# A rotary embedding whose tables are built from 64 partitions instead of 128, with the first unit loaded in one piece

## Chip, cores and metric

One core of a Trainium2 chip. The metric is the device time of one execution in microseconds (us). Each kernel was run several times, in turns with the kernel before on the same chip.

## The reference

```python
# x: (8, 8, 1024, 64) float32; cos_cached, sin_cached: (1024, 32) float32
x_first, x_second = x[..., :32], x[..., 32:]
out_first  = x_first * cos_cached - x_second * sin_cached
out_second = x_first * sin_cached + x_second * cos_cached
out = concatenate([out_first, out_second], axis=-1)
```

16.8 MB are read, 16.8 MB are written, and each element needs two products and one sum.

## The kernel before

x is cut into 8 units of 2 MB, each 128 partitions of 64 rows of 64 floats. Every partition needs one of 16 pieces of each table. The tables are therefore loaded once (128 KB each), and TensorE spreads them over the partitions by products with a selection matrix `sel` of zeros and ones; the results stand in PSUM banks `tp`. DVE takes its products on unit 0 straight from PSUM, while ACT copies the banks to SBUF (`tb`) for the units that follow. DVE makes nearly all products; POOL, TensorE and DVE share the sums; the SP queue loads and stores. In the profiles PE is TensorE, PEld its weight loads, DVE the vector engine, ACT the scalar engine and POOL the GpSimd engine. A table product sums over 128 rows of its operands; this sum is called its contraction.

```python
raw = sv[3][:, :BK]                               # BK = 512: 256 floats of sine, 256 of cosine
for eng, i, t in ((nc.sync, 0, sin_cached), (nc.scalar, 1, cos_cached)):
    eng.dma_start(out=raw[:, i * BK // 2:(i + 1) * BK // 2],
                  in_=t.rearrange("(q n) j -> q (n j)", q=P))       # 128 partitions of 1 KB
load(0, 0, F // 2)                                # unit 0 in two halves
load(0, F // 2, F)
for u in range(1, n_u - 1):
    load(u, 0, F)
gate = load(7, K * hd, F)
load(7, 0, K * hd)
...                                               # two short reads of x
sel = sv[3][:, BK:BK + N * P]
...                                               # POOL makes plus, the identity
nc.vector.tensor_copy(out=sel..., in_=plus...)    # 128 rows of selection
nc.scalar.mul(out=minus, in_=plus, mul=-1.0)
...
nc.tensor.matmul(tp[6][:, :BK], plus, ...)        # a preparatory product; its result is not used
for b, t in tp.items():                           # 8 table products, contraction over 128 rows
    for k in range(t.shape[1] // BK):
        nc.tensor.matmul(t[:, k * BK:(k + 1) * BK], sel[:, (b + k) * P:(b + k + 1) * P], rt,
                         start=True, stop=True)
...
keep(0, 1); on_pool(0, 0, B)                      # ACT copies, POOL takes 8 rows of unit 0
first(1, 1); keep(1, 1)                           # DVE: products on unit 0 from PSUM
first(2, 2); keep(2, 2)
first(4, 2); keep(4, 2)
first(6, 2); keep(6, 2)
for c, (u, n0, n1) in enumerate(chunks):          # units 1 to 7: products, sums, stores
    ...
```

Of the kernel before, what the change touches and what calls it, by code (L numbers as in the profile page):

```python
# [8 lines left out]
def kernel(  # L9
# [7 lines left out]
    nc = tc.nc  # L17
    fp32 = mybir.dt.float32
    TT = mybir.AluOpType
    P = nc.NUM_PARTITIONS  # L20

    b, h, seq, hd = x.shape
    half = hd // 2
    R = 64
    F = R * hd
    T = R * half
    n_u = (b * h * seq) // (R * P)
    BK = 512
    G = BK // half
    B = seq // P  # L30
    N = R // B
    S = P // N
# [9 lines left out]
    const = ctx.enter_context(tc.tile_pool(name="const", bufs=1))  # L42
# [5 lines left out]
    plus = const.tile([P, P], fp32, name="plus")  # L48
    minus = const.tile([P, P], fp32, name="minus")
# [4 lines left out]
    xt, sv, px = {}, {}, {}  # L54
# [17 lines left out]
    px[7] = both(w[:, F:F + 4 * L * hd])  # L72


    raw = sv[3][:, :BK]
    for eng, i, t in ((nc.sync, 0, sin_cached), (nc.scalar, 1, cos_cached)):
        eng.dma_start(out=raw[:, i * BK // 2:(i + 1) * BK // 2],  # L77
                      in_=t.rearrange("(q n) j -> q (n j)", q=P))


    def load(u, m0, m1):
        return nc.sync.dma_start(out=xt[u][:, m0:m1], in_=xf[u][:, m0:m1])  # L82

    load(0, 0, F // 2)
    load(0, F // 2, F)
    for u in range(1, n_u - 1):
        load(u, 0, F)
    gate = load(7, K * hd, F)
    load(7, 0, K * hd)


    row = const.tile([1, 2 * hd], fp32, name="row")
    for i in range(2):
        nc.sync.dma_start(out=row[:, i * hd:(i + 1) * hd], in_=xf[i][0:1, 0:hd])



    sel = sv[3][:, BK:BK + N * P]
    nc.gpsimd.memset(plus, 0.0)
    nc.gpsimd.affine_select(out=plus, in_=plus, compare_op=TT.not_equal, fill=1.0,  # L100
                            base=0, pattern=[[-1, P]], channel_multiplier=1)
    nc.vector.tensor_copy(  # L102
        out=sel.rearrange("q (k r j) -> q k r j", k=N, j=S),
        in_=plus.rearrange("q (j k) -> q k j", k=N).unsqueeze(2).to_broadcast([P, N, N, S]))
    nc.scalar.mul(out=minus, in_=plus, mul=-1.0)  # L105

    sn, cs = tb4[:, :, 0], tb4[:, :, 1]

# [55 lines left out]
    st, acc, q = {}, {}, []  # L164
# [44 lines left out]
    def put(c):  # L209
        if c < len(chunks):  # L210
# [10 lines left out]
           (4, 2, two, "left"), (6, 2, two, "left"))}  # L221
    nc.tensor.matmul(tp[6][:, :BK], plus, plus.unsqueeze(1).to_broadcast([P, BK // P, P]),  # L222
                     start=True, stop=True)
    rt = raw.rearrange("q (t n j) -> q n t j", t=2, j=half)
    for b, t in tp.items():
        for k in range(t.shape[1] // BK):
            nc.tensor.matmul(t[:, k * BK:(k + 1) * BK], sel[:, (b + k) * P:(b + k + 1) * P], rt,  # L227
                             start=True, stop=True)

    def first(b, n):  # L230
        products(xt[0][:, b * BK:(b + n) * BK], 0, b * B, (b + n) * B,
# [65 lines left out]
```

## Time and profile before

| | before |
|---|---|
| time | 85.07 us (85.02 to 85.11, 4 runs) |
| span of the profiled run | 83.2 us |
| DMA | 33.8 MB, near 430 GB/s from 4 to 81 us |
| first product of DVE and of POOL on unit 0 | 6.64 and 6.56 us |
| DVE's first product on unit 1 | 15.36 us |
| last store issued, landed | 74.7 us, 82.4 us |

### The profile page before, as it was taken

To read this page: it belongs to the slowest core of one execution; us is meant where nothing else is said; L and a number is where in the kernel's file an instruction comes from. 1 tells how busy PE (TensorE), PEld (TensorE's weight loads), DVE (VectorE), ACT (ScalarE), POOL (GpSimd) and SP (SyncE) were. 2 spreads that over 40 slices of the span, in tenths; PEclk is the share of its full clock that TensorE was granted. 3 is DMA by queue.
4 is the path that set the end of the run, shared out by engine and by line. 5 is a ranking of instruction groups with operands and counts; after the bars stand their busy time and mean duration, and the time that the engine had idled before them with its cause. 6 is when DMAs were issued, how large, how long until landed. Compare 5 with 4: busy or idle time off the path is not lost.

```text
span 83.2 us, 393 instructions
## 1 busy us (share of the span) xinstructions
PE 45.2 (54%) x82; PEld 17.4 (21%) x82; DVE 68.1 (82%) x30; ACT 38.1 (46%) x34; POOL 65.2 (78%) x38
## 2 busy tenths in 40 slices
PE   3999960009971952994962948909959800000000
PEld 2244410004411401341411404204304200000000
DVE  3105999899999999999999999999999999980000
ACT  4322048954467627666449383694049290000000
POOL 3008998799999999999999999999999969920000
PEclk9999999855599999579999999996599999555555
DMA  1999999999999999989999999999999999999991
GB/s 20 346 402 445 465 402 449 433 410 457 410 465 402 418 457 402 465 377 423 428 434 465 418 410 457 402 473 402 418 465 402 457 402 473 410 410 402 420 426 44
DMA packets 3172, 33.82 MB, mean 407 GB/s; under 512 B 356, under 2 KB 612, under 8 KB 1124
## 3 DMA queue, kind: packets, MB, share of 16 engines
q1 hardware_dynamic: 3028, 33.69, 95.9%
q10 hardware_dynamic: 144, 0.13, 0.5%
HBM read 17.04 MB, written 16.78 MB: 407 GB/s over the span
## 4 chain that ended last, share of the span: by engine, by line
DVE 45%; DMA 25%; issue 12%; ACT 4%; SPq 3%; DVEq 1%
DVE w L117 40%; DMA w<-in_x_dram 25%; ACT st L124 4%; DVE st L117 3%; SPq L82 2%; DVE w L120 1%; DVEq L292 1%; SPq L77 0%; DVEq L117 0%; DVEq L120 0%
## 5 line engine op out<-in xcount | busy, mean ns | idle before, releaser
L117 DVE TENSOR_TENSOR w<-st,tb 128x3072 f32<-128x3072 f32 (+3 forms) x19 | 53.1, 2869 | 0.5 <-ACT st L124 0.5
L124 ACT COPY st<-w 128x1536 f32<-128x1536 f32 (+1 forms) x19 | 24.8, 1309 | 16.0 <-DVE w L117 16.0
L176 PE MATMUL acc<-w,plus 128*128 128x512 f32 x32 | 20.1, 714 | 19.6 <-ACT w L182 12.5
L120 POOL TENSOR_TENSOR w<-w 128x1024 f32<-128x1024 f32 (+4 forms) x12 | 25.0, 2086 | 1.9 <-DVE w L117 1.7
L121 POOL TENSOR_TENSOR w<-w 128x1024 f32<-128x1024 f32 (+4 forms) x12 | 25.0, 2085 | 0.0
L117 POOL TENSOR_TENSOR w<-w,tb 128x1280 f32<-128x1280 f32 (+1 forms) x6 | 14.2, 2368 | 5.5 <-DMA w<-in_x_dram 5.3
L176 PEld LDWEIGHTS acc<-w,plus 128*128 128x128 f32 x32 | 6.5, 224 | 31.7 <-ACT w L182 18.3
L117 DVE TENSOR_TENSOR w<-w,tab 128x2048 f32<-128x2048 f32 (+1 forms) x4 | 7.9, 2018 | 4.7 <-PE tab L227 4.7
L177 PE MATMUL acc<-w,minus 128*128 128x512 f32 x16 | 10.8, 768 | 0.0
L182 ACT COPY w<-acc 128x1024 f32<-128x1024 f32 x8 | 8.1, 1008 | 5.6 <-PE acc L177 5.6
L227 PE MATMUL tab<-w 128*128 128x512 f32 x16 | 8.2, 669 | 0.1
L177 PE MATMUL acc<-w,plus 128*128 128x512 f32 x16 | 8.2, 592 | 0.0
L235 ACT COPY tb<-tab 128x1024 f32<-128x1024 f32 (+1 forms) x5 | 4.2, 840 | 7.9 <-DVE w L117 5.0
L177 PEld LDWEIGHTS acc<-w,minus 128*128 128x128 f32 x16 | 3.8, 236 | 5.0 <-issue 5.0
L227 PEld LDWEIGHTS tab<-w 128*128 128x128 f32 x16 | 3.5, 223 | 5.6 <-issue 5.6
L177 PEld LDWEIGHTS acc<-w,plus 128*128 128x128 f32 x16 | 3.2, 199 | 4.4 <-issue 4.4
L117 DVE TENSOR_TENSOR st<-st,tb 128x1024 f32<-128x1024 f32 (+1 forms) x2 | 3.0, 1489 | 0.0
L222 PE MATMUL tab<-plus 128*128 128x512 f32 x2 | 2.1, 1140 | 1.4 <-POOL plus L100 1.4
L102 DVE COPY w<-plus 128x1024 f32<-128x1024 f32 x1 | 1.1, 1099 | 1.3 <-POOL plus L100 1.3
L105 ACT ACT_TABLE_LOAD x1 | 1.3, 1283 | 1.2 <-PEq L281 1.2
L120 DVE TENSOR_TENSOR w<-st,w 128x512 f32<-128x512 f32 (+1 forms) x2 | 1.6, 825 | 0.1
L121 DVE TENSOR_TENSOR w<-st,w 128x512 f32<-128x512 f32 (+1 forms) x2 | 1.6, 815 | 0.0
(10 smaller groups left out, 3.2 us busy)
## 6 DMA issues: line engine op xcount, KB each, us to landing
out_dram<-w SPq DMA_DIRECT2D x7, 2048.0 KB, 11.7
w<-in_x_dram SPq DMA_DIRECT2D x6, 2048.0 KB, 26.8
w<-in_x_dram SPq DMA_DIRECT2D x2, 1024.0 KB, 6.3
out_dram<-w SPq DMA_DIRECT2D x2, 768.0 KB, 7.7
w<-in_x_dram SPq DMA_DIRECT2D x1, 1280.0 KB, 34.3
w<-in_x_dram SPq DMA_DIRECT2D x1, 768.0 KB, 33.7
out_dram<-w SPq DMA_DIRECT2D x1, 512.0 KB, 7.1
w<-in_cos_cached_dram ACTq DMA_DIRECT2D x1, 128.0 KB, 2.8
```

Source lines behind the costliest of these rows:

```text
L82: return nc.sync.dma_start(out=xt[u][:, m0:m1], in_=xf[u][:, m0:m1])
L105: nc.scalar.mul(out=minus, in_=plus, mul=-1.0)
L117: eng.tensor_tensor(out=o, in0=a, in1=t, op=TT.mult)
L120: eng.tensor_tensor(out=o[:, :, 0], in0=c[:, :, 0], in1=s[:, :, 1], op=TT.subtract)
L121: eng.tensor_tensor(out=o[:, :, 1], in0=c[:, :, 1], in1=s[:, :, 0], op=TT.add)
L124: nc.scalar.copy(out=pt[:, :(n1 - n0) * hd], in_=xt[u][:, n0 * hd:n1 * hd])
L176: nc.tensor.matmul(a[:, k], plus, xr[:, :, k], start=True, stop=False)
L177: nc.tensor.matmul(a[:, k], plus if k else minus, sr[:, :, 1 - k], start=False, stop=True)
L182: nc.scalar.copy(out=rows(xt[u], n0, n0 + G), in_=a)
L222: nc.tensor.matmul(tp[6][:, :BK], plus, plus.unsqueeze(1).to_broadcast([P, BK // P, P]), start=True, stop=True)
L227: nc.tensor.matmul(t[:, k * BK:(k + 1) * BK], sel[:, (b + k) * P:(b + k + 1) * P], rt, start=True, stop=True)
L235: nc.scalar.copy(out=tb[:, b * BK:(b + n) * BK], in_=tp[b])
```

## The change

Its intent, as far as the diff tells: fewer and larger pieces for the loads (tables in 2 KB instead of 1 KB, unit 0 in 16 KB instead of 8 KB), half the selection matrix, and less work for ACT. The third short read makes up for the load that was merged. In this diff, unchanged lines are left out and long ones are cut with `...`.

```diff
-    raw = sv[3][:, :BK]
+    Q = P // 2
+    raw = sv[3][:Q, :2 * BK]
     for eng, i, t in ((nc.sync, 0, sin_cached), (nc.scalar, 1, cos_cached)):
-        eng.dma_start(out=raw[:, i * BK // 2:(i + 1) * BK // 2],
-                      in_=t.rearrange("(q n) j -> q (n j)", q=P))
+        eng.dma_start(out=raw[:, i * BK:(i + 1) * BK],
+                      in_=t.rearrange("(q n) j -> q (n j)", q=Q))
-    load(0, 0, F // 2)
-    load(0, F // 2, F)
-    for u in range(1, n_u - 1):
+    for u in range(n_u - 1):
         load(u, 0, F)
-    row = const.tile([1, 2 * hd], fp32, name="row")
-    for i in range(2):
+    row = const.tile([1, 3 * hd], fp32, name="row")
+    for i in range(3):
-    sel = sv[3][:, BK:BK + N * P]
+    M = N // 2
+    sel = sv[3][:Q, 2 * BK:2 * BK + M * P]
     nc.vector.tensor_copy(
-        out=sel.rearrange("q (k r j) -> q k r j", k=N, j=S),
-        in_=plus.rearrange("q (j k) -> q k j", k=N)...)
-    nc.scalar.mul(out=minus, in_=plus, mul=-1.0)
+        out=sel.rearrange("q (k r j) -> q k r j", k=M, j=S),
+        in_=plus[:Q, :Q].rearrange("q (j k) -> q k j", k=M)...)
+    nc.gpsimd.tensor_scalar(out=minus, in0=plus, scalar1=-1.0, scalar2=None, op0=TT.mult)
-    rt = raw.rearrange("q (t n j) -> q n t j", t=2, j=half)
+    rt = raw.rearrange("q (t h n j) -> q h n t j", t=2, h=2, j=half)
-            nc.tensor.matmul(..., sel[:, (b + k) * P:(b + k + 1) * P], rt, ...)
+            nc.tensor.matmul(..., sel[:, (b + k) // 2 * P:((b + k) // 2 + 1) * P],
+                             rt[:, (b + k) % 2], ...)      # contraction over 64 rows
```

More of the change, by code (lines that the diff above doesn't have):

```diff
@@ L102 @@
     nc.vector.tensor_copy(
-        out=sel.rearrange("q (k r j) -> q k r j", k=N, j=S),
-        in_=plus.rearrange("q (j k) -> q k j", k=N).unsqueeze(2).to_broadcast([P, N, N, S]))
-    nc.scalar.mul(out=minus, in_=plus, mul=-1.0)
+        out=sel.rearrange("q (k r j) -> q k r j", k=M, j=S),
+        in_=plus[:Q, :Q].rearrange("q (j k) -> q k j", k=M).unsqueeze(2)
+        .to_broadcast([Q, M, N, S]))
+    nc.gpsimd.tensor_scalar(out=minus, in0=plus, scalar1=-1.0, scalar2=None, op0=TT.mult)
     sn, cs = tb4[:, :, 0], tb4[:, :, 1]
@@ L223 @@
                      start=True, stop=True)
-    rt = raw.rearrange("q (t n j) -> q n t j", t=2, j=half)
+    rt = raw.rearrange("q (t h n j) -> q h n t j", t=2, h=2, j=half)
     for b, t in tp.items():
         for k in range(t.shape[1] // BK):
-            nc.tensor.matmul(t[:, k * BK:(k + 1) * BK], sel[:, (b + k) * P:(b + k + 1) * P], rt,
-                             start=True, stop=True)
+            nc.tensor.matmul(t[:, k * BK:(k + 1) * BK], sel[:, (b + k) // 2 * P:((b + k) // 2 + 1) * P],
+                             rt[:, (b + k) % 2], start=True, stop=True)
     def first(b, n):
```

## The prediction

> **What bounds the kernel now.** I read the page's busy line and its slices first, because they say which engine has no slack left.
>
> ```profile
> PE 45.2 (54%) x82; PEld 17.4 (21%) x82; DVE 68.1 (82%) x30; ACT 38.1 (46%) x34; POOL 65.2 (78%) x38
> DMA  1999999999999999989999999999999999999991
> GB/s 20 346 402 445 465 402 449 433 410 457 410 465 402 418 457 402 465 377 423 428 434 465 418 410 457 402 473 402 418 465 402 457 402 473 410 410 402 420 426 44
> HBM read 17.04 MB, written 16.78 MB: 407 GB/s over the span
> ```
>
> DVE is busy 82% and the DMA row stands at 9 in 38 of 40 slices. The windows view gives the rate by stage (columns: stretch, its length, busy time of PE, PEld, DVE, ACT and POOL, PE clock, DMA share, GB/s).
>
> ```profile
> 1.50:2.00 0.50, 0.50 (x1) 0.36 (x2) 0.50 (x1) 0.50 (x1) 0.00 (x0) 1.00 0.73 68
> 2.00:2.50 0.50, 0.50 (x2) 0.00 (x0) 0.44 (x1) 0.49 (x2) 0.00 (x0) 1.00 0.57 193
> 4.00:9.00 5.00, 5.00 (x10) 2.06 (x10) 1.86 (x2) 1.17 (x2) 2.36 (x2) 1.00 1.02 423
> 9.00:20.00 11.00, 3.94 (x9) 1.65 (x8) 10.69 (x5) 6.86 (x6) 10.04 (x8) 0.82 1.01 432
> 70.00:76.00 6.00, 0.00 (x0) 0.00 (x0) 4.63 (x4) 0.00 (x0) 3.34 (x3) 0.55 1.01 431
> ```
>
> From 9 to 76 us the rate weighted over my stages is 430 GB/s, and never leaves 418 to 436 in a stage of 6 us or more. The 33.8 MB of loads and stores at 430 GB/s are 78.6 us, of a span of 83.2. The rest is the ramp up to about 2.5 us and some 1.5 us at the end, where the last packets land and the program closes.
>
> The chain of waits ends in DVE work at 74.66 us, which would make DVE the bound. But the timeline and the issues tell the rest: the last store is issued at 74.69 us, holds 768 KB (1.8 us at 430 GB/s) and yet takes 7.7 us to land.
>
> ```profile
> 73.80 0.86 DVEq L292
> 74.69 0.33 SPq L154 DMA_DIRECT2D out_dram<-w  x1
> out_dram<-w SPq DMA_DIRECT2D x1, 768.0 KB, 7.7
> out_dram<-w SPq DMA_DIRECT2D x1, 2048.0 KB, 9.9
> ```
>
> How long would it take alone? The first table load is issued at 0.74 us and its first packets move at about 1.7: 1.0 us to start. The last packets run near 81.7 us and the last landing is 74.69 + 7.7 = 82.4: 0.7 us to close. Alone it needs 1.0 + 1.8 + 0.7 = 3.5 us, so 4.2 us of the 7.7 is a queue of earlier stores. The smallest such reserve that I can read is that of unit 5's store, issued at 62.61 us (last line above): 9.9 - (1.0 + 4.9 + 0.7) = 3.3 us. The earlier 2 MB stores, with 11.5 to 12.2 us, have about 5. For unit 6's store I have no landing; counting bytes back from the last packet at 430 GB/s gives it 4.1 us ahead less 1.0 to start, 3.1 us. So **the DMA stream is the bound, and compute may come some 3 us later before a store arrives too late to keep the stream fed.**
>
> The front end of compute, where the change works, is in the waits and the timeline:
>
> ```profile
> POOL w L117 <- DMA w<-in_x_dram: 5.3, 1, 5.3
> DVE w L117 <- PE tab L227: 4.7, 2, 4.2
> 6.56 2.62 POOL L117 TENSOR_TENSOR w<-w,tb 128x512 f32<-128x512 f32 x2 [5.25 <-DMA w<-in_x_dram]
> 6.64 1.22 DVE L117 TENSOR_TENSOR w<-w,tab 128x1024 f32<-128x1024 f32 x1 [4.20 <-PE tab L227]
> 8.36 6.68 DVE L117 TENSOR_TENSOR w<-w,tab 128x2048 f32<-128x2048 f32 x3 [0.49 <-PE tab L227]
> ```
>
> POOL waits for the first half of unit 0, DVE for the tables from PE, and both start near 6.6 us. From 8.36 us on DVE hardly ever stops: its idle time before 74.66 us is only some 0.5 us.
>
> **What the Trainium skill says.** (1) "DMA: Bandwidth & Descriptors", section "Where 436 GB/s comes from", puts the ceiling at 435 GB/s for 16 ports; this trace's 430 agrees, so no arrangement of the loads raises the steady rate. (2) The same page, "Why small descriptors are slow (HBM only)", gives a fixed cost of about 3 cycles beside one cycle per 32 B. In the trace cos's queue spent 13.0% of 16 engines over 1 to 4 us on 144 packets: 43 ns each (16 of them tiny), where 1 KB at 430/16 GB/s is 38 ns. So about 5 ns a packet: agreement in kind. (3) "SBUF — State Buffer", section "Door 1: The DMA port swizzle", says that partitions 0 to 63 reach only 8 of the 16 ports and measured 196 GB/s for 64 partitions at 1 MiB. The tables move to 64 partitions, so this bears on the change; nothing in the trace before shows it. (4) "ScalarE: Activation LUTs", section "What ACT_TABLE_LOAD costs", gives 1283 ns for a table load; the trace has 1283 ns, ahead of the negation on ACT.
>
> **The change part by part.**
>
> *Tables in 64 partitions of 2 KB.* It removes 128 of 256 packets: 128 x 5 ns / 16 engines = 0.04 us of stream. More is in the ramp. Counted in steps of 0.2 us from 1.6, the trace has 9, 24, 15, 48, 75, 72 and 52 packets: engines are partly idle until 2.4, and x gets its full share only when the 256 table packets are through, near 3.0. If the ramp is paced by packets, 128 of them are through near 2.5 us. Then 0.26 MB of tables plus 0.5 us of x at 430 GB/s (0.21 MB) make 0.47 MB by 3.0 us, against 0.38 MB now: 0.09 MB, 0.2 us of stream. Against it stands the port rule: 0.26 MB at 196 GB/s is 1.3 us rather than 0.6. Much of that lies in the ramp, where only some 50 to 250 GB/s moved anyway, and x has packets for the other ports; I charge 0.1 us, at most 0.4.
>
> *The selection matrix halves in both directions.* The DVE copy goes from 1024 to 512 elements in a row, 1.10 to about 0.55 us, ended near 1.9 instead of 2.44. The table matmuls start at 3.58, when the tables have landed, so nothing follows. They stay 8 products of 512 columns, 16 instructions; half the rows of contraction should not change 0.43 to 0.85 us each.
>
> *Negation on POOL.* ACT loses 1.28 + 0.31 us before 2.8 us; its next work is at 5.67 us. POOL gains one 128x128 pass, about 0.3 us (its affine select of that shape took 0.29), near 1.3 us, and is idle till 6.56. The negative identity is first used near 20 us. Worth 0.
>
> *Unit 0 whole.* One issue of about 0.43 us less, and 128 packets of 16 KB for 256 of 8 KB: 0.04 us. But DVE and POOL now wait for the whole unit. Its second half landed at 1.65 + 7.3 = 8.95 us; the same bytes are ahead of it after, less the ramp's 0.2: about 8.7. DVE's first product then runs 8.75 to 9.97 us, and the second, which began at 8.36 because of PE, follows at once: **DVE 1.6 us later**. POOL: four operations of 4.1 us end at 12.9, sums of 3.7 end at 16.6, and the next sums need DVE's product that ended at 15.07, now 16.7: also 1.6 us later. Everything after moves by 1.6 us; the last store is issued at about 76.3. With reserves of 3.1 us or more this stays hidden, leaving 1.3 to 1.5 us.
>
> *Third short read.* 256 bytes. It replaces the load that was merged, so the loads stay 14 in number[...]. Worth 0.
>
> Sum on the path that sets the end: -0.2 (ramp) - 0.08 (packets) + 0.1 (ports) = -0.2 us: **84.9 us**.
>
> **The rivals.**
> *A: the delay of compute comes through.* For it: DVE has no idle time to absorb 1.6 us, and the chain of waits names DVE. Against it: 7.7 us of landing for a last store that needs 3.5. If I have the reserve at units 5 and 6 wrong by 2 us, some 0.5 us shows: 85.5; if the reserve were nil, 86.5.
> *B: the ports.* If the tables move at half rate while x is held up behind them, the stream loses 0.4 us net of the ramp gain: 85.3 to 85.5. For it: the skill's measured 196 GB/s. Against: the ramp is not bandwidth-bound, and tables are 0.8% of the bytes.
> *C: the ramp recovers more.* From 1.5 to 4 us the stream is some 0.8 us behind its steady rate. If more than half comes back, 84.4 to 84.6. Against: x's issue at 1.18 us does not move, so its first bytes cannot come much sooner.
> *D: the earlier table ends DVE's wait sooner.* No gain: DVE now waits for x, not PE, and is not the bound.
>
> **Range and chances.** A change of 2% is 1.7 us. Getting faster by that means removing more than the whole ramp, slower needs reserve nil. C's end is 84.4, B's and a mild A's 85.5: that is my range. Chances: faster 0.01, within 2% 0.97, slower 0.02.
>
> **What the profile after would show.** Right: POOL's and DVE's first product both released by the x load at about 8.7 us; the 0.49 us wait for PE gone; DVE's end and last issue near 76.3; its landing time down from 7.7 to about 6; the DMA row at 9 throughout; about 0.1 MB more moved by 3.0 us; no table load on ACT. Wrong: a dip in the DMA row between 62 and 76 us (A), tables landing later than 2.6 to 2.8 us after issue (B), a last issue that moved much less or more than 1.6 us.

## The result

The changed kernel takes **86.19 us** (86.02 to 86.37, 4 runs), against 85.07: a ratio of 1.0132, 95% interval 1.0108 to 1.0155. Ratios here are the mean time of one kernel's fast runs over that of the other's of the same rounds, so not quite the ratio of the quoted medians. The prediction said 84.9 us with a range of 84.4 to 85.5: wrong in direction, and outside its range. Its chance of 0.97 for a change within 2% came true.

**Where the time went.** The page of the changed kernel:

```profile
DMA  0999999999999999989999999999999688989993
...
GB/s 7 326 395 434 426 442 426 426 442 426 442 426 442 418 434 411 449 376 436 426 452 434 426 442 426 442 418 434 418 442 418 256 372 372 496 372 401 403 420 140
```

The row that stood at 9 throughout has a dip at about 66 to 70 us. The windows view (columns as in the prediction) shows the hole, before ahead of after:

```profile
60.00:70.00 10.00, 5.19 (x11) 1.69 (x10) 9.80 (x8) 5.75 (x5) 9.09 (x5) 0.98 1.00 426
67.00:68.00 1.00, 0.00 (x0) 0.00 (x0) 1.00 (x2) 1.00 (x2) 0.65 (x1) 1.00 1.04 442
```

```profile
60.00:70.00 10.00, 7.84 (x14) 3.33 (x15) 9.89 (x7) 5.40 (x6) 10.00 (x5) 0.83 0.87 372
67.00:68.00 1.00, 0.55 (x2) 0.31 (x3) 0.96 (x2) 1.00 (x2) 1.00 (x2) 1.00 0.01 0
```

From 67 to 68 us not a byte moves. The missing 54 GB/s over 10 us are 0.54 MB, or 1.26 us at 430 GB/s. The issues of the changed kernel say why: unit 4's store was issued at 61.07 us and landed 6.7 us later, about what such a store needs alone by the prediction's sum (6.6 us), so nothing was ahead of it; unit 5's was issued only at 67.47 us, 4.9 us later than before (62.61), when the queue had run dry.

```profile
61.07 0.33 SPq L155 DMA_DIRECT2D out_dram<-w  x1
out_dram<-w SPq DMA_DIRECT2D x1, 2048.0 KB, 6.7
...
67.47 0.33 SPq L155 DMA_DIRECT2D out_dram<-w  x1
```

A smaller share went at the start. From 1.5 to 9 us the stream moved 358 GB/s instead of 376: 0.135 MB, or 0.3 us. The two together are about 1.6 us; the spans differ by 1.4.

**Who is late.** The chain of waits of the changed kernel (start, length, what) now begins with something that was not in it before:

```profile
0.71 3.29 DMA w<-in_cos_cached_dram
4.01 0.09 issue
4.10 14.00 PE tab L228 x16
18.10 0.02 issue
18.12 0.03 DVE w L118
```

The table products take 14 us. The groups of the two pages (line, engine, operation, shapes, count, busy us, mean ns, idle before) say it side by side, before and after:

```profile
L227 PE MATMUL tab<-w 128*128 128x512 f32 x16 | 8.2, 669 | 0.1
```

```profile
L228 PE MATMUL tab<-w 64*128 64x512 f32 x16 | 14.0, 1065 | 0.7 <-DMA w<-in_cos_cached_dram 0.7
```

The same number of instructions with the same 512 columns takes 8.2 us with 128 rows and 14.0 with 64. (The mean of one overstates it, since a matmul's modelled end overlaps the next; busy time over count, or the distance of the starts, is the rate.) The weight loads of TensorE in the timeline give the distances, before and after:

```profile
5.42 0.34 PEld L227 LDWEIGHTS tab<-w 128*128 128x128 f32 x1 [0.52 <-issue]
6.01 0.19 PEld L227 LDWEIGHTS tab<-w 128*128 128x128 f32 x1 [0.25 <-issue]
6.44 0.19 PEld L227 LDWEIGHTS tab<-w 128*128 128x128 f32 x1 [0.24 <-issue]
```

```profile
14.47 0.33 PEld L228 LDWEIGHTS tab<-w 64*128 64x128 f32 x1 [0.52 <-issue]
15.32 0.33 PEld L228 LDWEIGHTS tab<-w 64*128 64x128 f32 x1 [0.52 <-issue]
16.18 0.33 PEld L228 LDWEIGHTS tab<-w 64*128 64x128 f32 x1 [0.52 <-issue]
```

Before, TensorE starts with 0.85 us from one instruction to the next and goes over to 0.43 us at 6.0 us. After, it stays at 0.85 us to the last table product, at 18 us, though it has been busy without a pause since 4.1 us. The row of the granted clock is no help here: both pages show 9 in it over all this time, and the mean granted clock of the runs with 64 rows is even the higher one (0.89 to 0.92, against 0.84 to 0.86 before). The distances are the evidence.

DVE's products on unit 0 follow TensorE's pace. Three of them now wait for it, 3.0 us in all, on top of the wait for the whole of unit 0 that was predicted:

```profile
9.31 1.22 DVE L118 TENSOR_TENSOR w<-w,tab 128x1024 f32<-128x1024 f32 x1 [7.38 <-DMA w<-in_x_dram]
11.30 2.29 DVE L118 TENSOR_TENSOR w<-w,tab 128x2048 f32<-128x2048 f32 x1 [0.77 <-PE tab L228]
...
14.71 2.29 DVE L118 TENSOR_TENSOR w<-w,tab 128x2048 f32<-128x2048 f32 x1 [1.13 <-PE tab L228]
...
18.12 2.29 DVE L118 TENSOR_TENSOR w<-w,tab 128x2048 f32<-128x2048 f32 x1 [1.13 <-PE tab L228]
```

Unit 1 starts on DVE at 20.33 us instead of 15.36: 5.0 us late, not 1.6.

### The profile page after: what moved, and what is told of

It reads as the page before. It is cut to its first block, busy times and chain, and to the rows that moved or that the text cites. A ratio compares the mean times of both kernels' runs of the same rounds, so it can differ in the third digit from the quotient of the medians.

```text
span 84.6 us, 391 instructions
## 1 busy us (share of the span) xinstructions
PE 50.4 (60%) x82; PEld 19.0 (23%) x82; DVE 67.7 (80%) x30; ACT 37.7 (45%) x33; POOL 66.1 (78%) x39
## 4 chain that ended last, share of the span: by engine, by line
DVE 43%; PE 17%; issue 15%; DMA 11%; ACT 6%; DVEq 1%; SPq 0%
DVE w L118 40%; PE tab L228 17%; DMA out_dram<-w 7%; ACT st L125 5%; DMA w<-in_cos_cached_dram 4%; DVE st L118 2%; DVE w L121 1%; ACT w L183 1%; DVEq L293 1%; DVEq L118 0%; SPq L155 0%; DVEq L121 0%
## 5 line engine op out<-in xcount | busy, mean ns | idle before, releaser
L228 PE MATMUL tab<-w 64*128 64x512 f32 x16 | 14.0, 1065 | 0.7 <-DMA w<-in_cos_cached_dram 0.7
L178 PE MATMUL acc<-w,minus 128*128 128x512 f32 x16 | 10.3, 735 | 0.0
L228 PEld LDWEIGHTS tab<-w 64*128 64x128 f32 x16 | 5.2, 330 | 9.5 <-issue 9.5
L236 ACT ACT_TABLE_LOAD x1 | 1.3, 1283 | 1.3 <-PEq L282 1.3
L102 DVE COPY w<-plus 64x512 f32<-64x512 f32 x1 | 0.6, 614 | 1.3 <-POOL plus L100 1.3
```

Of the source, the lines that this page charges most:

```text
L102: nc.vector.tensor_copy(out=sel.rearrange("q (k r j) -> q k r j", k=M, j=S), in_=plus[:Q, :Q].rearrange("q (j k) -> q k j", k=M).unsqueeze ...
L178: nc.tensor.matmul(a[:, k], plus if k else minus, sr[:, :, 1 - k], start=False, stop=True)
L228: nc.tensor.matmul(t[:, k * BK:(k + 1) * BK], sel[:, (b + k) // 2 * P:((b + k) // 2 + 1) * P], rt[:, (b + k) % 2], start=True, stop=True)
L236: nc.scalar.copy(out=tb[:, b * BK:(b + n) * BK], in_=tp[b])
```

## The experiments

**The theory (A).** Products that contract over 64 rows do not bring TensorE to its faster rate; the tables come late, DVE falls 5.0 us behind, the reserve of the stores (3 us and a little) is overrun, and the stream has a hole. **Rivals.** B: it is the wait for the whole of unit 0. A2: it is not the rows, but the idle gap of 0.7 us before the table products (the tables land later), which lost a warm-up that the preparatory product had begun.

### e1_tables_back: the tables alone put back

```diff
 # the changed kernel, with raw, sel, rt and the matmul as in the kernel before:
-    raw = sv[3][:Q, :2 * BK]
+    raw = sv[3][:, :BK]                          # 128 partitions of 1 KB, 128 rows
```

> The changed kernel with the tables alone put back into 128 partitions of 1 KB (128-row contraction); unit 0 whole, POOL negation and third read stay. Theory A (the table products on 64 rows keep TensorE at 0.85 us per instruction, DVE's first products wait for them, and the 4.9 us delay overruns the reserve of stores): table products fall to 0.43 us by about 8 us, DVE starts unit 1 some 2 to 2.7 us later than before (reserve 3.1 us), no gap in the stream, 84.9 to 85.2 us. Rival B (waiting for the whole of unit 0 is what costs): stays at 85.9 to 86.3 us.

Measured: 84.87 us (84.69 to 85.08, 6 runs), ratio to before 0.999, interval 0.9971 to 1.001: not to be told from before. The table products go over to 0.43 us at 7.75 us, and DVE's four products on unit 0 run without a wait for TensorE, once the unit is there (the timeline):

```profile
8.92 7.81 DVE L115 TENSOR_TENSOR w<-w,tab 128x1024 f32<-128x1024 f32 x4 [6.51 <-DMA w<-in_x_dram]
16.96 6.62 DVE L115 TENSOR_TENSOR w<-st,tb 128x3072 f32<-128x3072 f32 x2 [0.23 <-ACT st L122]
```

Unit 1 starts at 16.96 us, 1.6 us later than before, which is just what the prediction had worked out for unit 0 loaded whole, and it costs nothing. From 60 to 70 us the stream moves 429 GB/s. So unit 0 whole, the negation on POOL and the third read together cost no measurable time. B falls.

### e2_tables_only: the kernel before with the tables alone changed

```diff
 # the kernel before, with raw, sel, rt and the matmul of the changed kernel; unit 0 in halves
-    raw = sv[3][:, :BK]
+    raw = sv[3][:Q, :2 * BK]                     # 64 partitions of 2 KB, 64 rows
```

> The kernel before with the tables alone changed (64 partitions, 64-row contraction); unit 0 in halves, ACT negation, two reads stay. Theory A: table products stay at 0.85 us to about 18 us, DVE's last product on unit 0 ends near 20.4 us as in the changed kernel although unit 0 comes in halves, 86.0 to 86.4 us. Rival B: 85.0 to 85.3 us.

Measured: 86.52 us (86.17 to 86.78, 4 runs), ratio 1.0182, interval 1.0153 to 1.021: as theory A has it, 0.1 us above its range. The products take 14.0 us again. DVE starts unit 0 at 8.13 us, earlier than in the changed kernel, and has lost that by its last product on unit 0, which starts at 18.38 us, right after the last table product. The table part makes the whole loss by itself, and with it in place it does not matter how unit 0 arrives.

### e3_pad_128: 64 partitions of table, 128 rows of contraction

The loads stay as in the changed kernel. The lower 64 rows are zero in both operands, so TensorE computes the same sums.

```diff
-    raw = sv[3][:Q, :2 * BK]
+    raw = sv[3][:128, :2 * BK]
+    nc.vector.memset(raw[Q:], 0.0)
-        eng.dma_start(out=raw[:, i * BK:(i + 1) * BK],
+        eng.dma_start(out=raw[:Q, i * BK:(i + 1) * BK],
-    sel = sv[3][:Q, 2 * BK:2 * BK + M * P]
+    sel = sv[3][:128, 2 * BK:2 * BK + M * P]
-        in_=plus[:Q, :Q]...to_broadcast([Q, M, N, S]))
+        in_=plus[:128, :Q]...to_broadcast([128, M, N, S]))
```

> The changed kernel, same table loads into 64 partitions, but the contraction runs over 128 rows, the lower 64 zero on both sides (DVE zeroes them early). Theory A1 (64 active rows do not bring TensorE to its faster rate): products fall to 0.43 us by about 8 us although the idle gap of 0.7 us before them stays; total 85.1 to 85.4 us, the slower start of the loads (some 0.3 us) remaining. Rival A2 (the 0.7 us gap before the table products, waiting for the table load, lost the warm-up): products stay at 0.85 us, 86.0 to 86.4 us.

Measured: 85.34 us (85.13 to 85.62, 6 runs), ratio 1.005, interval 1.0029 to 1.0072. The group of the table products:

```profile
L230 PE MATMUL tab<-w 128*128 128x512 f32 x16 | 9.1, 733 | 0.7 <-DMA w<-in_cos_cached_dram 0.7
```

The gap of 0.7 us ahead of them is still there, and they go over to 0.43 us at 8.35 us all the same. So it is the number of rows that the instruction takes, not the gap, and not what the rows hold: half of them are zeros. The remaining 0.5% comes up again below.

### e4_no_gap: 64 rows, without the gap

```diff
+    nc.tensor.matmul(tp[6][:, :BK // 2], plus,
+                     plus.unsqueeze(1).to_broadcast([P, BK // P // 2, P]), start=True, stop=True)
```

> The changed kernel with half a preparatory product more (128 rows, 256 columns, two instructions of about 0.43 us), so that TensorE is busy without a gap from 1.3 us until the table products, still on 64 rows. A1 (rows): products stay at 0.85 us or fall back to it, 86.0 to 86.4 us. A2 (gap): products fall to 0.43 us by about 7 us, 85.1 to 85.5 us.

Measured: 86.26 us (86.24 to 87.04, 4 runs), ratio 1.0184, interval 1.0144 to 1.0224. TensorE is now busy from 1.34 to 18.2 us without a pause, and the weight loads of the table products stay 0.85 us apart throughout:

```profile
L230 PE MATMUL tab<-w 64*128 64x512 f32 x16 | 14.0, 1067 | 0.0
```

A2 falls from both sides.

### e5_pad_96: 96 rows

As e3 with 96 in the place of 128 (32 rows of zeros).

> As e3, but contraction over 96 rows (32 of them zero). Only the length of the table products counts. If any full-looking activity is enough: 0.43 us by about 8 us as in e3, about 85.3 us. If TensorE needs more than 96 of the rows: 0.85 us to the end, about 86.2 us.

One run, state unknown: 85.46 us. The products go over to 0.43 us at 9.14 us. So somewhere above 64 rows and at or below 96 lies what was enough here, by one profile.

### e6_delay_1 and e7_delay_2: the reserve by itself

If the reserve is real, the kernel before should bear a delay of DVE up to some 3 us for nothing and pay for more. No table, load or TensorE instruction is touched.

```diff
+    pb = plus.unsqueeze(1).to_broadcast([P, 16, P])
+    for i in range(1):                            # 2 in e7_delay_2
+        mul(nc.vector, sv[1][:, :16 * P].rearrange("p (k j) -> p k j", k=16), pb, pb)
     for c, (u, n0, n1) in enumerate(chunks):
```

> The kernel before with one useless DVE product of 2048 elements a row (about 2.28 us, into a buffer that is free then) between unit 0 and unit 1; everything else as before. If the stores have a reserve of 3.1 to 3.3 us: DVE and the stores 2.0 us later, stream without a gap, 84.9 to 85.2 us. If compute is the bound, as the chain of waits has it: 87.0 us.

Measured: 85.14 us (84.84 to 85.18, 4 runs), ratio 1.0002, interval 0.9986 to 1.0018. DVE starts unit 1 at 17.65 us, 2.3 us later than before, and nothing is lost:

```profile
17.65 3.36 DVE L117 TENSOR_TENSOR w<-st,tb 128x3072 f32<-128x3072 f32 x1
```

By unit 5's store the delay has shrunk to 1.6 us (64.16 against 62.61). The result refutes the chain of waits of the kernel before, which had led to DVE.

> The same with two such products: DVE 4.3 us later. Reserve of 3.1 to 3.3 us: the end moves by the part over it, 1.0 to 1.2 us, 86.0 to 86.3 us, with a gap in the stream between unit 4's and unit 5's stores. Compute as the bound: 89.3 us. Fully hidden: 85.0 us.

Measured: 87.53 us (87.02 to 87.82, 4 runs), ratio 1.0274. More than expected, because the dose was not what I had meant: the two products took 6.6 us rather than 4.6, and POOL's sums beside them 4.3 and 4.4 us instead of 2.35. The two held each other up. (In e6 one of POOL's two sums had taken 4.3 us already.) Besides, TensorE had gone over to 0.43 us only at 8.0 us in this profile. DVE started unit 1 at 22.79 us, 7.4 us late, and the stream stands still from 62 to 64 us.

### e10_delay_psum: the dose again, without that collision

```diff
     first(6, 2)
     keep(6, 2)
+    for i in range(4):
+        mul(nc.vector, sv[1][:, :8 * P].rearrange("p (k j) -> p k j", k=8),
+            tp[6].rearrange("p (k j) -> p k j", k=8), plus.unsqueeze(1).to_broadcast([P, 8, P]))
```

> The kernel before with four useless DVE products of 1024 elements a row (1.22 us each, one operand read from PSUM, so that they do not collide with POOL as the second product of the run before did) between unit 0 and unit 1: DVE 4.6 to 4.9 us later, as in the changed kernel, with TensorE fast and the loads untouched. Reserve of 3.1 to 3.3 us: a gap in the stream ahead of unit 5's store and 86.2 to 86.6 us. If something else of the changed kernel was needed for its loss: 85.0 to 85.3 us.

Measured: 87.09, 87.91 and 86.97 us in the fast runs (one slow run is left out), ratio 1.027, interval 1.0228 to 1.0312. The four products took 5.0 us as meant, and POOL's sums beside them 2.33 us each, so the collision is gone. But they waited 1.3 us for ACT and held up ACT's next copy, so unit 1 starts at 21.33 us, 6.0 us late. Twice the dose came out too high; the order is clear nevertheless. Part of e10's loss is not of this kind: its time is 2.5 to 2.6 us longer than the span of its core, where every other run here has 1.7 to 1.9. Where these 0.7 us come from was not looked into; by the spans of its fast runs (84.5, 85.4 and 84.5 us against 83.2) e10 loses 1.6 us. The runs on one scale, with the delay of DVE's start on unit 1 against the 15.36 us of before:

| kernel | TensorE in the table products | delay of unit 1 on DVE | unit 5's store issued | ratio to before |
|---|---|---|---|---|
| e1_tables_back | 0.43 us from 7.75 us on | 1.6 us | 64.2 us | 0.999 |
| e3_pad_128 | 0.43 us from 8.35 us on | 2.2 us | 64.8 us | 1.005 |
| e6_delay_1 | 0.43 us from 6.76 us on | 2.3 us | 64.2 us | 1.0002 |
| changed kernel | 0.85 us | 5.0 us | 67.5 us | 1.0132 |
| e4_no_gap | 0.85 us | 5.1 us | 67.4 us | 1.0184 |
| e2_tables_only | 0.85 us | 5.2 us | 67.8 us | 1.0182 |
| e10_delay_psum | 0.43 us from 5.95 us on | 6.0 us | 66.9 us | 1.027 |
| e7_delay_2 | 0.43 us from 8.00 us on | 7.4 us | 68.6 us | 1.0274 |

Up to 2.3 us there is no loss that goes with the delay, and from 5.0 us on there is one, whether TensorE was slow or a useless product held DVE up. The exact edge of the reserve was not measured; it lies between. In e7 and e10 the hole opens already ahead of unit 4's store, which was issued at 63.74 and 62.08 us instead of 56.11, so unit 5's store doesn't put these two in order.

The second column shows one thing more. Up to the table products e6, e7 and e10 are the kernel before, which went over at 6.01 us: the moment varies by 2 us between runs of the same instructions, so it says nothing about 96 rows against 128. But in all eleven profiles with 96 or 128 rows TensorE went over, and in none of the three with 64.

### e8_both_halves, e11_pad_again, e12_halves_again: the slower start

e3 has a fast TensorE and yet stays 0.5% above before. Its loads are those of the changed kernel. DVE's delay of 2.2 us is hardly the reason: from 60 to 70 us its stream moves 437 GB/s, without a hole. Either 64 partitions take the tables up more slowly (P, the ports of the prediction's rival B), or the loads of 2 KB pieces are slower to get under way (I). e8 puts sine into partitions 0 to 63 and cosine into 64 to 127:

```diff
+    raw = sv[3][:, :2 * BK]
+    nc.vector.memset(raw[:Q, BK:], 0.0)
+    nc.vector.memset(raw[Q:, :BK], 0.0)
-        eng.dma_start(out=raw[:, i * BK:(i + 1) * BK],
+        eng.dma_start(out=raw[i * Q:(i + 1) * Q, i * BK:(i + 1) * BK],
 # and sel filled in both halves from plus[i * Q:(i + 1) * Q, i * Q:(i + 1) * Q]
```

> The changed kernel, still 2 KB pieces, but sine in partitions 0 to 63 and cosine in 64 to 127, zeros in the other places, contraction over 128 rows. It has the fast TensorE of e3, and asks why e3 stays 0.5 us above e1. Theory P[...]: tables land as early as in e1, stream at e1's level, 84.8 to 85.0 us. Theory I (a table load of 64 pieces of 2 KB is itself issued more slowly, 0.54 against 0.38 us, and holds up x): as e3, 85.2 to 85.5 us.

Measured: 85.09 us (85.05 to 85.23, 5 runs), ratio 1.0007, interval 0.9994 to 1.0019. That lies between the two ranges, nearer to P's; but e3 had run on another chip, and e8's own profile has 350 GB/s from 1.5 to 9 us, below e1's 385. So both were run again side by side:

> The padded kernel of e3 again, beside the next on the same chip, since the two were measured on different chips. Theory P (half the ports): 0.4 to 0.6% above before, and 0.3 to 0.5% above the next. Theory I (slow issue of 2 KB pieces): no difference to the next.

> The kernel of e8 again (sine in partitions 0 to 63, cosine in 64 to 127), for the comparison with the run before. Theory P: 0.0 to 0.1% above before. Theory I: 0.3 to 0.5% above before.

Measured: e11 (half the partitions) 85.31 us, ratio 1.0032, interval 1.0012 to 1.0052; e12 (both halves) 85.24 us, ratio 1.0021, interval 1.0003 to 1.004. On the same chip the two are not to be told apart. The profiles agree with that. The windows view from 1.5 to 9 us, for before, e1, e11 and e12:

```profile
1.50:9.00 7.50, 7.35 (x12) 2.86 (x13) 2.81 (x3) 2.42 (x4) 2.36 (x2) 1.00 0.99 376
```

```profile
1.50:9.00 7.50, 7.32 (x10) 2.75 (x11) 0.98 (x2) 1.50 (x2) 1.34 (x2) 1.00 0.97 385
```

```profile
1.50:9.00 7.50, 6.93 (x9) 2.57 (x10) 1.02 (x2) 1.67 (x2) 0.41 (x1) 1.00 0.95 354
```

```profile
1.50:9.00 7.50, 7.09 (x10) 2.73 (x11) 1.71 (x3) 1.67 (x2) 0.40 (x1) 1.00 0.94 352
```

Tables in 1 KB pieces: 376 and 385 GB/s. In 2 KB pieces: 354 and 352, whether both tables go to one half of the partitions or one to each. 22 to 24 GB/s over 7.5 us is 0.17 to 0.18 MB, some 0.4 us at 430 GB/s; timed, it is 0.2 to 0.3% on this chip and 0.5% for e3. In the timelines the issue of a 2 KB table load takes longer, before and after:

```profile
0.74 0.38 SPq L77 DMA_DIRECT2D w<-in_sin_cached_dram  x1
```

```profile
0.72 0.54 SPq L78 DMA_DIRECT2D w<-in_sin_cached_dram  x1
```

The first load of x is issued at 1.32 instead of 1.18 us, and the first packets move at 2.0 instead of 1.7 us. I fits the profiles. For P speaks that the tables land later, as rival B had it: cosine 3.3 us after its issue in the changed kernel and 3.2 in e11, against 2.8 before and 3.0 in e12, and the longer issue is only some 0.16 us of that. Against P speaks what the packets took. From 1 to 4 us those of cosine's queue (packets, MB, share of 16 engines' time) were, before and after:

```profile
q10 hardware_dynamic: 144, 0.13, 13.0%
```

```profile
q10 hardware_dynamic: 80, 0.13, 12.2%
```

That is 6.2 and 5.9 us of engine time for the same table; at half the rate it would have been about twice as much. So a halved rate is refuted for these loads. A smaller effect is not: e8 and e12, too, send each single load to one half of the partitions, and no run sends 2 KB pieces to all 128. Why 64 pieces of 2 KB take longer to issue than 128 of 1 KB was not found, and why e8's timed ratio was as low as 1.0007 stays open too.

### e9_x_first: a try for more

```diff
-    for eng, i, t in ((nc.sync, 0, sin_cached), (nc.scalar, 1, cos_cached)):
+    for eng, i, t in ((nc.scalar, 0, sin_cached), (nc.scalar, 1, cos_cached)):
```

> A try for a faster version: the kernel before with both table loads issued by ACT, so that the first load of x is issued by SP at 0.73 instead of 1.18 us. The stream would start some 0.4 us earlier: 84.5 to 84.8 us, if the tables, now sharing the engines with x, land no more than 3 us later than before. If they land later, DVE falls behind the reserve: above 85.3 us.

Measured: 87.36 to 88.41 us in five fast runs (a slow one is left out), ratio 1.0317, interval 1.0281 to 1.0352. The tables landed 5.9 and 8.3 us after their issue instead of 2.6 and 2.8, most likely because x is now under way beside them from the first. The stream was no further for it: 374 GB/s from 1.5 to 9 us, against 376. The table products started at 9.6 us, and DVE was 7.6 us late on unit 1: again beyond the reserve.

No kernel beats the one before measurably. e1 is level with it.

## Why the prediction was wrong

- **What bounds the kernel: right.** Transfers set the end, compute has a reserve, and unit 5's store has among the least of it. e6 shows the reserve, and the hole in the changed kernel opens right ahead of unit 5's store. The size of some 3 us stays an estimate, which the hole supports: 4.9 us of delay of that store less 1.3 us of hole are 3.6.
- **Unit 0 whole: right, in size too.** DVE 1.6 us later was predicted; e1 has 1.6 us, and no loss. In e1, the change without its table part, the rest of that forecast holds as well: the last store is issued at 76.30 us (76.3 predicted) and lands 5.8 us later (about 6 predicted).
- **The failed step** is in the paragraph on the selection matrix: "half the rows of contraction should not change 0.43 to 0.85 us each", and with it that the second product of DVE "follows at once". An instruction of 64 rows is indeed no slower than one of 128 in the same state of TensorE: 0.85 us. But I took for granted that the change from 0.85 to 0.43 us, which the kernel before makes at 6 us, would come again. With 64 rows it did not come in 14 us of unbroken work; with 96 or 128 it did, 4.2 to 5.2 us after the first table product in e1, e3, e5 and e8. That put TensorE on the path of DVE, with its last product at 18.1 us instead of 11.8. The delay became 5.0 us instead of 1.6, which is more than the reserve.
- **Rival A** ("the delay of compute comes through") is what happened, in kind. I had weighed it as a mistake in the reserve; the mistake was in the delay. **Rival D** took for granted that the tables would be ready earlier and that DVE would wait for x alone; they were ready later, and DVE waited 3.0 us for TensorE.
- **The ramp: wrong in sign.** A gain of 0.2 us was predicted from fewer packets; 0.3 us were lost by 9 us, with the table loads issued more slowly and the first packets 0.3 us later. The first load of x, which rival C took as fixed at 1.18 us, moved to 1.32. **Rival B**, the ports, named a loss of that size, and its sign, tables landing later, did appear. But cosine's packets took no more engine time than before, and e11 and e12 are not to be told apart: no halved rate. Whether the ports have a smaller part in the 0.3 us stays open.
- **The negation on POOL: no cost, as said, but mis-sized.** The pass takes 0.96 us in the changed kernel and 1.44 us in e1, not 0.3. And ACT's table load did not go: it now stands before ACT's first copy, still 1283 ns, and still off the path.

About four fifths of the loss, 1.26 of about 1.6 us, is the hole in the stream; the rest is the start.

## What to carry to other kernels

When a change halves the rows that a product contracts over (here from 128 to 64, in float32), do not count on TensorE's faster rate: look at the distance of its instructions, not at the clock row, and if the work is on someone's path, pad the rows with zeros. And when a stream of transfers hides compute, work out the reserve of each store first, as landing time less what the store needs alone, and then hold every delay of the change, summed, against it.

## What the Trainium skill lacked or had wrong

- **TensorE: Matmul & The Clock Gate, section "What's actually happening"**, says that activity releases the throttle, after about 3.4 us of sustained work. It doesn't say that the rows of contraction count. Here 14 us of unbroken products over 64 rows stayed at 0.85 us each (changed kernel, e2, e4), while 96 rows (e5) and 128 rows, half of them zeros (e3), came to 0.43 us within 4.2 to 5.2 us.
- **SBUF — State Buffer, section "Door 1: The DMA port swizzle"**, says that 64 partitions get no more DMA bandwidth than 32, since they reach the same ports. For table loads of 128 KB beside a stream, no halved rate shows here: cosine's packets took 5.9 us of engine time in partitions 0 to 63 and 6.2 in all 128 (changed kernel and before).
- **DMA: Bandwidth & Descriptors, section "Rules for kernel authors"**, advises to coalesce small transfers into larger ones, and leaves open, in its note on the tile shape, whether few large pieces or many small ones are faster for the same bytes. Here 64 pieces of 2 KB took 0.54 to 0.55 us to issue and 128 of 1 KB took 0.38 to 0.39 us, and the stream was some 0.4 us behind by 9 us (e11 and e12 against before).
